# Feed-forward heads whose matmuls take w1 and w3 together, in units that hold two chunks of rows of both

## The chip, the cores and the metric

The kernel runs on one core of one Trainium2 chip. The metric is the device time of one execution in microseconds (us), less is better. Engines are named as in the profile: PE (TensorE, matmuls), PEld (its weight loads), DVE (VectorE), ACT (ScalarE), POOL (GpSimd) and SP (SyncE, which here only issues DMAs).

## The reference

One inference step of a diffusion backbone of two layers, on 384 tokens of 1024 numbers: 128 context tokens and 256 latent tokens, which is three tiles of 128 here. Each layer is a feed-forward half (FFN1), a token mixer (Fourier mixing, latent attention, neighbourhood attention, merged by gates and projected by `w_out`), and a second feed-forward half (FFN2). What the change touches is the feed-forward:

```python
def _modulate(x, shift, scale):
    return (_ln_plain(x) * (1.0 + scale) + shift)

def _swiglu(h, w1, w3, w2):                 # w1, w3: 1024 x 2816, w2: 2816 x 1024
    return (jax.nn.silu(h @ w1) * (h @ w3)) @ w2

def _ffn_sublayer(x, shift, scale, gate, w1, w3, w2, g, b):
    y = _swiglu(_modulate(x, shift, scale), w1, w3, w2)
    return _layernorm(ALPHA * x + 0.5 * gate * y, g, b)
```

All is fp32. The kernel splits each fp32 operand of a product into a high and a low part (fp32r) and adds three matmuls: high by high, high by low, low by high.

## The kernel before

The program is a row of sublayers: FFN1, mixer, FFN2, twice. Between two of them stands `transition(prev, nxt, mod)`: the old sublayer's last matmuls tile by tile (`tail(t)`: for a mixer the product with the eight chunks of `w_out`, tile `wo`; for a feed-forward the last eight chunks of w2, tile `y`), each followed by `res(t)` (gate, residual, layer norm; tiles `z`, `st`, and a square on ACT into `xn`), `norm(t)` (second normalisation; POOL's power into `st`, then `xn` on DVE) and `modu(t)` (transposes `xT` on PE, scale and shift into `hf` on DVE and ACT, then the split into `hmh` on ACT and `hml` on DVE). `modu(0)` stands within the last tail; `res(2)` and `norm(2)` ahead of the head; `modu(1)` and `modu(2)` after the first piece of the heads of tiles 0 and 1.

The **head** of a feed-forward is what follows: the first 512 of the 2816 columns of w1 and w3, in two groups `g` of 256, with the tokens as the stationary operand and the weights moving. For tile t and group g one PSUM bank `hd` holds h @ w1 in its first 256 columns and h @ w3 in its last 256; `sf` is then silu of the one times the other. The remaining columns come later, in `body`, with the weights stationary. The first sublayer of all has a head of its own (`cold_head`), which the change doesn't touch. The heads in question are three: T1 (mixer to FFN2, layer 0), T2 (FFN2 of layer 0 to FFN1 of layer 1) and T3 (mixer to FFN2, layer 1).

**Units and the planner.** Weights come in units. A unit is loaded by SP as raw fp32 (`raw`, line 180), cast by ACT to the high part (`whi`, line 188), and DVE subtracts to get the low part (`wlo`, line 193); each of the three takes a slot. There are two kinds of slot: `NU4` = 26 of 4 KB a partition and `NT3` = 22 of 3 KB; what has 768 words or fewer a partition goes into a 3 KB slot. Residual tiles, rows of the layer norm and gate, scratch tiles and most weight units take 4 KB slots. A first pass over the program, without emitting, notes when each unit is first and last used and a planned clock; `make_plan` and `place` then choose, unit by unit in order of first use, at which matmul its load and its two conversions are emitted: as early as wished (a lookahead in planned us) and as there is room among the slots in all the time until its last use. Conversions keep the order of first use. Where a unit finds no room, the lookahead of it and the ten before it shrink, and all is placed again:

```python
            for r in range(max(0, bad - 10), bad + 1):
                la[r] = (la[r][0] * 0.7, la[r][1] * 0.85)
```

SP issues its loads in the order in which they stand; one that waits for its slot (for the last reader of what was in it) holds up those behind it, and each also waits until the DMA eight before it has landed, on whose semaphore it counts. ACT, DVE and PE also run in program order.

Of the kernel before, what the change touches and what calls it, by code (L numbers as in the profile page):

```python
# [16 lines left out]
P = 128  # L17
D = 1024
KD = 8
# [1245 lines left out]
class FFN:  # L1265
# [13 lines left out]

    def w13(self, nme, g, c):  # L1280
        l, f, k = self.l, self.f, self.k
        n = 3 if g == 0 else 4
        i = c // n
        w = k.W((nme, l, f, g, i), f"ffn{f}_{nme}", l, i * n * P, min(n, KD - i * n), g * 256, 256)
        return tuple(x[:, c % n] for x in w)

    def head(self, t):
        k, nc = self.k, self.k.nc
        c = slice(t * P, (t + 1) * P)

        def piece(g, i):
            def go():
                if i == 0:
                    self.hb[t, g] = k.psum("hd")
                    if t == 0:
                        self.sf[g] = k.slot([P, NT, 256], F32, "sf")
                b = self.hb[t, g]
                for kk in range(KD):
                    k.mm3(b[:, i * 256:i * 256 + 256], (k.hm[0][:, kk, c], k.hm[1][:, kk, c]),
                          self.w13(("w1", "w3")[i], g, kk), kk == 0, kk == KD - 1)  # L1300
                if i == 1:
                    sf = self.sf[g][:, t]
                    nc.scalar.activation(out=sf, in_=b[:, 0:256], func=AF.Silu)
                    nc.vector.tensor_tensor(out=sf, in0=b[:, 256:512], in1=sf, op=ALU.mult)
            return go
        return [piece(g, i) for g in range(HG) for i in range(2)]
# [203 lines left out]
```

## Time and profile before

| | |
|---|---|
| median of 3 runs | 1886.09 us |
| lowest and highest | 1885.56 and 1888.81 us |
| the profiled execution | 1885.24 us |
| its span, first to last instruction | 1883.4 us |
| its mean granted PE clock | 0.997 |
| PE, PEld busy | 99%, 92% of the span |
| DVE, ACT, POOL busy | 71%, 42%, 7% of the span |
| DMA, mean over the span | 170 GB/s |

The busy time of PE is modelled from pipelined matmuls, so its share says that PE always has something, not that it is at its peak; how long a run of matmuls takes is read from the chain of waits, where the pieces follow each other. A timeline's row gives the start of an instruction or of a group of the same, its length, the engine, the line, the tiles and a count, and in brackets the idle time before it and what ended that. Line 77 is a helper that records most operations; tiles tell them apart.

### The profile page before, as it was taken

The page shows a single profiled execution, that of the slowest core. Times are in us where ns is not written, and L with a number is a line of the kernel's source. Part 1 is how long each engine was busy: PE and PEld are TensorE (multiplying, and loading weights), DVE is VectorE, ACT ScalarE, POOL GpSimd, SP SyncE. Part 2 cuts the span into 40 slices and gives each one's busy share as a digit, 9 for nine tenths or more (in the row PEclk, how much of TensorE's full clock was granted, in tenths as well). Part 3 has the DMA queues.
Part 4 walks back from the last instruction along what each step waited for, and adds up shares of the span by engine and source line. Part 5 has one row for each costly group of instructions (what it writes and reads, how often), then busy time and mean ns, then how long its engine had stood idle before and what let it go on. Part 6 is the DMA issues. An engine that isn't in the chain of part 4 may idle for free. (4 is left out here: it accounts for less than half of the span.)

```text
span 1883.4 us, 27546 instructions
## 1 busy us (share of the span) xinstructions
PE 1859.8 (99%) x10651; PEld 1726.4 (92%) x10651; DVE 1332.3 (71%) x2100; ACT 789.3 (42%) x1318; POOL 136.3 (7%) x287
## 2 busy tenths in 40 slices
PE   7999999999999999999999999999999999999997
PEld 5899998999999999999899999899999998999996
DVE  5776877688886676768775868778796876533344
ACT  4433335555365453323452333355554553533330
POOL 0000102000200000001000100220001000000000
PEclk9999999999999999999999999999999999999999
DMA  9865665234734456657555666543365354344522
GB/s 307 286 217 197 214 213 196 89 102 139 227 114 170 124 168 212 207 196 226 177 164 184 212 215 221 196 144 93 112 195 153 113 187 138 123 134 123 145 90 78
DMA packets 226243, 320.23 MB, mean 170 GB/s; under 512 B 33424, under 2 KB 182528, under 8 KB 225984
## 3 DMA queue, kind: packets, MB, share of 16 engines
q1 hardware_dynamic: 223616, 313.89, 51.9%
q0 software_dynamic: 2496, 4.59, 0.6%
q8 instruction: 83, 1.36, 0.3%
q14 instruction: 48, 0.39, 0.1%
HBM read 312.32 MB, written 8.02 MB: 170 GB/s over the span
## 5 line engine op out<-in xcount | busy, mean ns | idle before, releaser
L193 DVE TENSOR_TENSOR wlo<-raw,whi 128x1024 fp32r<-128x1024 f32 (+4 forms) x420 | 491.4, 1186 | 160.5 <-ACT whi L188 74.3
L188 ACT CAST whi<-raw 128x1024 fp32r<-128x1024 f32 (+4 forms) x420 | 421.1, 1021 | 369.3 <-DVE wlo L193 119.6
L77 PE MATMUL w<-hmh,whi 128*128 128x384 f32 x1152 | 386.7, 336 | 0.5 <-DVE sl L77 0.5
L77 PE MATMUL w<-hmh,wlo 128*128 128x384 f32 x1152 | 385.5, 335 | 0.0
L77 PE MATMUL w<-hml,whi 128*128 128x384 f32 x1152 | 385.2, 334 | 0.0
L77 PE MATMUL y<-whi,sT 128*128 128x512 f32 x1056 | 337.8, 391 | 0.7 <-DVE sT L77 0.4
L77 DVE SCALAR_TENSOR_TENSOR acc<-raw,cs,acc 128x1024 f32<-128x1024 f32 x236 | 295.3, 1286 | 11.9 <-DMA raw<-in_w_ada_dram 10.4
L77 PEld LDWEIGHTS y<-whi,sT 128*128 128x128 f32 x1056 | 197.9, 188 | 43.0 <-DVE sT L77 1.1
L77 PEld LDWEIGHTS w<-hmh,whi 128*128 128x128 f32 x1152 | 216.3, 188 | 12.1 <-issue 5.0
L77 PEld LDWEIGHTS w<-hml,whi 128*128 128x128 f32 x1152 | 216.3, 188 | 1.9
L77 PEld LDWEIGHTS w<-hmh,wlo 128*128 128x128 f32 x1152 | 216.2, 188 | 0.0
L77 PE MATMUL y<-wlo,sT 128*128 128x512 f32 x528 | 206.3, 391 | 0.0
L77 PE MATMUL g<-hmh,whi 128*128 128x384 f32 x384 | 131.9, 343 | 0.0
L77 PE MATMUL g<-hml,whi 128*128 128x384 f32 x384 | 129.1, 336 | 0.0
L77 PE MATMUL g<-hmh,wlo 128*128 128x384 f32 x384 | 129.1, 336 | 0.0
L77 PEld LDWEIGHTS y<-wlo,sT 128*128 128x128 f32 x528 | 99.1, 188 | 19.4
L77 ACT CAST sT<-sl 128x384 fp32r<-128x384 f32 x72 | 37.0, 514 | 159.8 <-DVE sl L77 159.8
L77 PE MATMUL hd<-whi,hmh 128*128 128x256 f32 (+1 forms) x336 | 101.1, 303 | 0.9 <-ACT hmh L77 0.7
L77 PE MATMUL hd<-wlo,hmh 128*128 128x256 f32 (+1 forms) x336 | 99.9, 299 | 0.0
L77 PE MATMUL hd<-whi,hml 128*128 128x256 f32 (+1 forms) x336 | 99.7, 299 | 0.0
L77 POOL TENSOR_TENSOR st<-st,mhalf 128x1 f32<-128x1 f32 x48 | 43.4, 906 | 662.9 <-DVE st L77 661.7
L77 DVE TENSOR_TENSOR sl<-w,sl 128x384 f32<-128x384 f32 x72 | 39.8, 553 | 52.3 <-PE w L77 52.0
(262 smaller groups left out, 2935.7 us busy)
## 6 DMA issues: line engine op xcount, KB each, us to landing
raw<-in_ffn_w_dram SPq DMA_DIRECT2D x244, 512.0 KB, 4.7
raw<-in_w_ada_dram SPq DMA_DIRECT2D x128, 512.0 KB, 5.0
raw<-in_w_gate_dram SPq DMA_DIRECT2D x48, 512.0 KB, 4.6
raw<-in_w_in_dram SPq DMA_DIRECT2D x32, 512.0 KB, 6.4
raw<-in_w_out_dram SPq DMA_DIRECT2D x16, 512.0 KB, 6.7
raw<-gd SPq DMA_DIRECT2D x12, 512.0 KB, 5.3
raw<-in_ffn_w_dram SPq DMA_DIRECT2D x22, 256.0 KB, 4.9
raw<-in_ffn_w_dram SPq DMA_DIRECT2D x12, 384.0 KB, 8.3
```

What stands on the lines that cost most here:

```text
L77: r = f(*a, **kw)
L188: self.real.scalar.copy(out=hi, in_=r)
L193: self.real.vector.tensor_tensor(out=lo, in0=r, in1=hi.bitcast(F32), op=ALU.subtract)
```

## The change

`w13` loses its case for group 0: its units all have four chunks now, and it serves the body alone. A new function `both(g, kk)` makes the head's units: each holds chunks 2i and 2i+1 of rows, of w1 and of w3, 256 columns each (2 x 2 x 256 = 1024 words a partition), filled by two DMAs of 256 KB, one from w1 and one from w3. Of the head's two pieces for a tile and a group, the first was w1 over all eight chunks and the second w3; now the first is chunks 0 to 3 and the second chunks 4 to 7, and each matmul writes all 512 columns of the bank. For a head that is 144 matmuls of 512 columns in the place of 288 of 256. Before, a head's ten units were, for group 0, six of three, three and two chunks of w1 and the same of w3 (768 or 512 words, 3 KB slots), and for group 1 four of four chunks (4 KB slots); now there are eight, all in 4 KB slots. In the program SP has 721 DMAs where it had 703, and ACT and DVE have two casts and two subtracts less per head.

```diff
@@ -1279,10 +1279,19 @@
 
     def w13(self, nme, g, c):
         l, f, k = self.l, self.f, self.k
-        n = 3 if g == 0 else 4
-        i = c // n
-        w = k.W((nme, l, f, g, i), f"ffn{f}_{nme}", l, i * n * P, min(n, KD - i * n), g * 256, 256)
-        return tuple(x[:, c % n] for x in w)
+        w = k.W((nme, l, f, g, c // 4), f"ffn{f}_{nme}", l, c // 4 * 4 * P, 4, g * 256, 256)
+        return tuple(x[:, c % 4] for x in w)
+
+    def both(self, g, kk):
+
+        l, f = self.l, self.f
+        i = kk // 2
+
+        def src(o):
+            return [((lambda t, x=x: t[:, :, x]), o.I[f"ffn{f}_{n}"][l, i * 2 * P:(i + 1) * 2 * P, g * 256:g * 256 + 256].rearrange("(a p) b -> p a b", p=P))
+                    for x, n in enumerate(("w1", "w3"))]
+        w = self.k.unit(("both", l, f, g, i), src, (2, 2, 256), True)
+        return tuple(x[:, kk % 2].rearrange("p a b -> p (a b)") for x in w)
 
     def head(self, t):
         k, nc = self.k, self.k.nc
@@ -1295,9 +1304,8 @@
                     if t == 0:
                         self.sf[g] = k.slot([P, NT, 256], F32, "sf")
                 b = self.hb[t, g]
-                for kk in range(KD):
-                    k.mm3(b[:, i * 256:i * 256 + 256], (k.hm[0][:, kk, c], k.hm[1][:, kk, c]),
-                          self.w13(("w1", "w3")[i], g, kk), kk == 0, kk == KD - 1)
+                for kk in range(4 * i, 4 * i + 4):
+                    k.mm3(b, (k.hm[0][:, kk, c], k.hm[1][:, kk, c]), self.both(g, kk), kk == 0, kk == KD - 1)
                 if i == 1:
                     sf = self.sf[g][:, t]
                     nc.scalar.activation(out=sf, in_=b[:, 0:256], func=AF.Silu)
```

The planner places the new units elsewhere. On SP at T1 there stood, before, the last three of the six units of group 0, then a unit of group 1, then the second and third residual rows (`xd`), then two units of group 1:

```order
L180 DMA raw_1174_6441<-in_ffn2_w3_dram 128x3x256
L180 DMA raw_1187_6475<-in_ffn2_w3_dram 128x3x256
L180 DMA raw_1188_6481<-in_ffn2_w3_dram 128x2x256
L180 DMA raw_1189_6486<-in_ffn2_w1_dram 128x4x256
L180 DMA raw_1190_6505<-xd_533_2955 128x1024
L180 DMA raw_1216_6624<-xd_534_2957 128x1024
L180 DMA raw_1217_6627<-in_ffn2_w1_dram 128x4x256
L180 DMA raw_1218_6629<-in_ffn2_w3_dram 128x4x256
```

Now the eight pairs stand between the second and the third residual row, of which these are the last four (raw_1200 holds chunks 0 and 1 of group 0, which PE needs first):

```order
L180 DMA raw_1199_6595<-in_ffn2_w1_dram 128x2x256
L180 DMA raw_1199_6595<-in_ffn2_w3_dram 128x2x256
L180 DMA raw_1200_6601<-in_ffn2_w1_dram 128x2x256
L180 DMA raw_1200_6601<-in_ffn2_w3_dram 128x2x256
L180 DMA raw_1201_6604<-in_ffn2_w1_dram 128x2x256
L180 DMA raw_1201_6604<-in_ffn2_w3_dram 128x2x256
L180 DMA raw_1202_6610<-in_ffn2_w1_dram 128x2x256
L180 DMA raw_1202_6610<-in_ffn2_w3_dram 128x2x256
L180 DMA raw_1203_6622<-xd_534_2957 128x1024
```

All the head's loads moved behind the second residual row, and the third residual row and the first-needed pair stand near their end.

On ACT at T1, before, six casts stand ahead of the residual steps (`xn` from `z` is a square for a variance, `hf` and `hmh` are the modulation of tile 0):

```order
L77 CAST mT_1163_6374<-g_1161_6357 128x384
L188 CAST whi_1191_6522<-raw_1171_6421 128x768
L188 CAST whi_1193_6531<-raw_1172_6428 128x768
L188 CAST whi_1205_6562<-raw_1173_6435 128x512
L188 CAST whi_1208_6587<-raw_1174_6441 128x768
L188 CAST whi_1210_6596<-raw_1187_6475 128x768
L188 CAST whi_1212_6604<-raw_1188_6481 128x512
L77 ACTIVATE xn_1178_6453,st_1177_6451<-z_1175_6445,st_1177_6451 128x1024
L77 ACTIVATE xn_1182_6463,st_1181_6461<-z_1175_6445,st_1181_6461 128x1024
L77 ACTIVATE xn_1198_6544,st_1197_6542<-z_1195_6536,st_1197_6542 128x1024
L77 ACTIVATE hf_1203_6557<-xT_1207_6567,mod_876_4681 128x128 x2
```

Now no cast of the head stands ahead of the modulation of tile 0:

```order
L77 ACTIVATE xn_1174_6445,st_1173_6443<-z_1171_6437,st_1173_6443 128x1024
L77 ACTIVATE xn_1178_6455,st_1177_6453<-z_1171_6437,st_1177_6453 128x1024
L77 ACTIVATE xn_1187_6522,st_1186_6520<-z_1184_6514,st_1186_6520 128x1024
L77 ACTIVATE hf_1192_6535<-xT_1194_6541,mod_876_4681 128x128 x2
L77 CAST hmh_1_65<-hf_1192_6535 128x4x128
L77 ACTIVATE hf_1192_6535<-xT_1194_6541,mod_876_4681 128x128 x2
L77 CAST hmh_1_65<-hf_1192_6535 128x4x128
L188 CAST whi_1204_6626<-raw_1200_6601 128x1024
L188 CAST whi_1206_6632<-raw_1196_6583 128x1024
L77 ACTIVATE xn_1209_6639,st_1208_6637<-z_1184_6514,st_1208_6637 128x1024
L77 ACTIVATE xn_1215_6654,st_1214_6652<-z_1212_6646,st_1214_6652 128x1024
L188 CAST whi_1220_6668<-raw_1197_6587 128x1024
```

The cast of the first-needed pair stands right behind it, and the casts of the later pairs behind the squares of tiles 1 and 2. On PE, the head of T1 began before with chunk 0 of w1 (whi_1191 is the cast of raw_1171):

```order
L77 MATMUL wo_1202_6553<-wlo_1158_6319,mT_1163_6374 128x512
L77 MATMUL wo_1202_6553<-whi_1157_6318,mT_1163_6374 128x512
L77 MATMUL hd_1236_6690<-whi_1191_6522,hmh_1_65 128x256
L77 MATMUL hd_1236_6690<-wlo_1192_6523,hmh_1_65 128x256
L77 MATMUL hd_1236_6690<-whi_1191_6522,hml_2_66 128x256
```

Now it begins with both matrices at once:

```order
L77 MATMUL wo_1191_6531<-wlo_1165_6388,mT_1159_6366 128x512
L77 MATMUL wo_1191_6531<-whi_1164_6387,mT_1159_6366 128x512
L77 MATMUL hd_1218_6662<-whi_1204_6626,hmh_1_65 128x512
L77 MATMUL hd_1218_6662<-wlo_1205_6627,hmh_1_65 128x512
L77 MATMUL hd_1218_6662<-whi_1204_6626,hml_2_66 128x512
```

The stationary tiles and their order are the same; the moving operand is twice as wide, and comes from the pair loaded sixth. On SP at T3, before, the loads of group 0 stand ahead of all rows and the order there is:

```order
L180 DMA raw_2679_15242<-in_ffn2_w3_dram 128x3x256
L180 DMA raw_2682_15257<-in_ffn2_w3_dram 128x2x256
L180 DMA raw_2683_15263<-in_ffn2_w1_dram 128x4x256
L180 DMA raw_2689_15322<-xd_2058_11924 128x1024
L180 DMA raw_2690_15324<-gd_1854_10785 128x1024
L180 DMA raw_2691_15326<-gd_1854_10785 128x1024
L180 DMA raw_2692_15328<-in_ln_g_dram 128x1024
L180 DMA raw_2693_15330<-in_ln_b_dram 128x1024
L180 DMA raw_2720_15434<-in_ffn2_w1_dram 128x4x256
L180 DMA raw_2721_15437<-xd_2059_11926 128x1024
L180 DMA raw_2733_15501<-in_ffn2_w3_dram 128x4x256
```

Now the pairs come after the second residual row:

```order
L180 DMA raw_2687_15118<-xd_2047_11630 128x1024
L180 DMA raw_2696_15148<-in_ffn2_w1_dram 128x2x256
L180 DMA raw_2696_15148<-in_ffn2_w3_dram 128x2x256
L180 DMA raw_2700_15183<-in_ffn2_w1_dram 128x2x256
L180 DMA raw_2700_15183<-in_ffn2_w3_dram 128x2x256
L180 DMA raw_2701_15188<-in_ffn2_w1_dram 128x2x256
L180 DMA raw_2701_15188<-in_ffn2_w3_dram 128x2x256
L180 DMA raw_2702_15197<-in_ffn2_w1_dram 128x2x256
L180 DMA raw_2702_15197<-in_ffn2_w3_dram 128x2x256
L180 DMA raw_2703_15206<-in_ffn2_w1_dram 128x2x256
L180 DMA raw_2703_15206<-in_ffn2_w3_dram 128x2x256
```

There raw_2702 holds chunks 0 and 1 of group 0, raw_2703 chunks 2 and 3, raw_2700 chunks 4 and 5 and raw_2701 chunks 6 and 7; raw_2696 belongs to group 1. At T2 the order is of the same kind: eight pairs in a row, and the first-needed is the fifth.

## Rows read from the trace of the kernel before

**Rows 1.** the page's part 1: busy us (share of the span) xinstructions

```profile
PE 1859.8 (99%) x10651; PEld 1726.4 (92%) x10651; DVE 1332.3 (71%) x2100; ACT 789.3 (42%) x1318; POOL 136.3 (7%) x287
```

**Rows 2.** PE's waits: who waited for whom, us, times, longest

```profile
PE hd L77 <- ACT hmh L77: 0.7, 1, 0.7
```

**Rows 3.** chain of waits, 1560 to 1660: start us, us, what

```profile
1595.82 2.87 PE hd L77 x24
1598.70 0.87 PE xT L77 x8
1599.57 11.51 PE hd L77 x96
```

**Rows 4.** chain of waits, 1181 to 1262, a run of 512-column matmuls

```profile
1248.78 5.48 PE uf L77 x24
```

**Rows 5.** timeline of SP (T1, T3): start us, us, what, xcount

```profile
665.00 0.34 SPq L180 DMA_DIRECT2D raw<-xd  x1
665.45 5.75 SPq L180 DMA_DIRECT2D raw<-in_ffn_w_dram  x6
...
1524.77 6.77 SPq L180 DMA_DIRECT2D raw<-in_ffn_w_dram  x6
...
1587.79 0.38 SPq L180 DMA_DIRECT2D raw<-in_ffn_w_dram  x1
1590.87 0.33 SPq L180 DMA_DIRECT2D raw<-xd  x1
```

**Rows 6.** timeline of PE: first hd matmul of T1 and T2

```profile
669.56 0.28 PE L77 MATMUL hd<-whi,hmh 128*128 128x256 f32 x1
...
953.49 0.28 PE L77 MATMUL hd<-whi,hmh 128*128 128x256 f32 x1
```

**Rows 7.** timeline of ACT, T3: start us, us, what, xcount

```profile
1563.95 4.08 ACT L188 CAST whi<-raw 128x768 fp32r<-128x768 f32 x6
```

**Rows 8.** groups by line and form: busy us, mean ns, idle before

```profile
L193 DVE TENSOR_TENSOR wlo<-raw,whi 128x1024 fp32r<-128x1024 f32 x376 | 455.7, 1225 | 160.3 <-ACT whi L188 74.1 <-PE w L77 29.8 <-issue 27.4
L188 ACT CAST whi<-raw 128x1024 fp32r<-128x1024 f32 x376 | 390.0, 1052 | 362.0 <-DVE wlo L193 117.9 <-PE w L77 80.7 <-DVE acc L77 61.7
...
L77 POOL TENSOR_TENSOR st<-st,mhalf 128x1 f32<-128x1 f32 x48 | 43.4, 906 | 662.9 <-DVE st L77 661.7 <-DVE sel L77 1.1
...
L77 DVE SCALAR_TENSOR_TENSOR z<-z,st,raw 128x1024 f32<-128x1024 f32 x30 | 38.4, 1279 | 2.0 <-POOL st L77 1.4 <-DMA raw<-in_ffn_w_dram 0.3
...
L77 DVE TENSOR_SCALAR hf<-xT,mod 128x128 f32<-128x128 f32 x60 | 20.9, 402 | 2.4 <-PE xT L77 2.4
...
L77 DVE TENSOR_TENSOR hml<-hf,hmh 128x512 fp32r<-128x512 f32 x30 | 20.2, 685 | 2.8 <-ACT hmh L77 2.4
...
L77 ACT CAST hmh<-hf 128x512 fp32r<-128x512 f32 x30 | 18.2, 620 | 2.6 <-DVE hf L77 2.3
...
L77 DVE TENSOR_SCALAR xn<-z,st,st 128x1024 f32<-128x1024 f32 x15 | 12.2, 813 | 8.1 <-POOL st L77 8.1
...
L77 DVE TENSOR_TENSOR sf<-hd,sf 128x256 f32<-128x256 f32 x24 | 9.5, 417 | 12.3 <-ACT sf L77 12.3
...
L77 DVE SCALAR_TENSOR_TENSOR z<-wo,raw 128x512 f32<-128x512 f32 x12 | 8.1, 687 | 9.0 <-PE wo L77 8.9
```

**Rows 9.** all DMA issues: KB each, median us to landing

```profile
raw<-in_ffn_w_dram SPq DMA_DIRECT2D x22, 256.0 KB, 4.9
raw<-in_ffn_w_dram SPq DMA_DIRECT2D x12, 384.0 KB, 8.3
...
raw<-in_w_branch_m_dram SPq DMA_DIRECT2D x8, 512.0 KB, 4.0
```

**Rows 10.** windows, T3: us, busy PE PEld DVE ACT POOL, PEclk, DMA, GB/s

```profile
1595.60:1612.00 16.40, 16.40 (x139) 16.36 (x139) 13.48 (x27) 7.86 (x15) 2.00 (x2) 1.00 0.69 226
```

**Rows 11.** windows: the kernel's end; columns as in rows 10

```profile
1870.00:1875.00 5.00, 3.90 (x18) 2.89 (x16) 1.68 (x3) 0.00 (x0) 0.00 (x0) 1.00 0.00 0
...
1880.00:1883.00 3.00, 0.00 (x0) 0.00 (x0) 0.00 (x0) 0.00 (x0) 0.00 (x0) 0.50 0.27 98
```

## Prediction

> **What bounds the kernel now.** I read the page's first part first: TensorE (PE) is busy 1859.8 us of 1883.4, VectorE (DVE) 71%, ScalarE (ACT) 42% [rows 1]. Then PE's waits: of all the head matmuls (tile hd) one waited, for 0.7 us [rows 2]. Then the chain of waits, which through the heads is PE alone: hd matmuls back to back, with only the xT transposes between them [rows 3]. So before the change every weight of a head is there in time, and two things decide: how long PE needs for a head, and whether the weights and the modulated tiles still come in time once their loads and conversions stand elsewhere.
>
> **PE's own gain.** A run of 96 hd matmuls of 256 columns takes 11.51 us [rows 3], 0.1199 us each. A matmul of 512 columns takes 5.48/24 = 0.2283 us [rows 4]. Two become one: 2 x 0.1199 - 0.2283 = 0.0115 us. Each head has 3 tiles x 2 column groups x 2 matrices x 8 chunks x 3 products = 288 matmuls of 256 that become 144 of 512; three heads change (mixer to second FFN in layer 0, second FFN to the next layer's first, mixer to second FFN in layer 1; T1, T2, T3 below). 432 x 0.0115 = 4.9 us saved, all on the path. A page speaks to the size: the Trainium skill, "TensorE: Matmul & The Clock Gate", Part 1, section "Wait — 56ns, not 53.3ns?", gives a matmul at full clock a fixed cost of about 2.5 ns beside its columns. By that the saving would be 432 x 2.5 ns, an estimate of 1.1 us, and the sum 3.8 us higher; the row says more than four times as much, and I go by the row.
>
> **What the planner does with the new units.** Before, each head's first column group came in six units of 768 or 512 words a partition, which live in the 22 slots of 3 KB, apart from the 26 slots of 4 KB that everything else crowds into. In T3, for example, they were loaded from 1524.77 on [rows 5] and cast from 1563.95 on [rows 7] for a head that begins at 1595.82 [rows 3]; the heads of T1 and T2 begin at 669.56 and 953.49 [rows 6]. Now all eight units of a head have 1024 words and want three 4 KB slots each while rows, residual tiles and the last w_out or w2 chunks still hold these. The order shows the result: in T1 all eight units' loads, each now two DMAs, stand behind the second residual row, and the pair that PE needs first (raw_1200, chunks 0 and 1) is the sixth; ACT's six early casts are gone, and the casts stand after the modulation of tile 0. In T2 the pair needed first is the fifth. In T3 it is the fourth, and the pair needed second the fifth. Two conversions less per head (1.05 + 1.23 us each [rows 8]) are work off the path; I give them nothing beyond the count below.
>
> **When the first pair comes.** SP waits for each slot's last reader, and the loads behind it wait too. In T1 and T2 the slots come free one by one as the last 24 matmuls of the tail read their chunks for the last time. The first is free 21 matmuls before the head, 21 x 0.228 = 4.8 us: at 664.8 in T1, where the old kernel's xd load, waiting for the matmul beside it, went out at 665.00, the next 0.45 later [rows 5], and at 948.7 in T2. Three pairs go ahead, six issues of 0.45 = 2.7 us; the needed pair's second DMA is one more behind: 667.9 and 951.9. Landing takes a median of 4.9 us for 256 KB [rows 9]: 672.8 and 956.8; the cast 1.05 [rows 8]. First matmul at 673.9 and 957.8 against 669.56 and 953.49: 4.3 us late each. Bounds: the quickest weight loads land in 4.0 us, the 384 KB loads, which come in bursts as these will, in 8.3 [rows 9]: 3.4 to 7.7 us late. I take 4.9, the row of the same size. In T3 the first pair waits for what released the 1587.79 load [rows 5] and is in time; the second waits, as the xd load at 1590.87 did: 1591.3 + 4.9 + 1.05 = 1597.25.
>
> **What DVE then has to do.** From the first cast on, before tile 1's matmuls can begin, DVE must run, in this order of program: 8 subtracts (8 x 1.225 = 9.8), four half-row residual steps (4 x 0.69 = 2.75), two layer-norm steps (2 x 1.28 = 2.56), xn of tile 1 (0.81), the four modulation steps that fall to it (4 x 0.40 = 1.61) and sf (0.42): 17.95 us, then ACT's cast hmh (0.62): 18.6 us [rows 8]. PE's work over that stretch is 48 matmuls x 0.2283 + 0.87 for xT [rows 3, 4] = 11.84. So 6.7 us are lost, whatever the loads do: DVE becomes the bound of the first third of the head. Before, most of these subtracts lay ahead, and DVE was already busy 13.48 of 16.40 us there [rows 10]; with four more subtracts it would need 18.4, more than the stretch has. Behind it xn of tile 2 (POOL 0.91 + DVE 0.81, against a cast and two matmuls, 1.08) costs 0.65 and hml (2 x 0.69 against 0.87) 0.5: 1.1 us. In T3 DVE may start at 1594.15, 1.5 us ahead of PE's first need, but stands idle from 1595.4 to 1597.25 for the second pair: 6.7 - 1.5 + 1.85 + 1.1 = 8.2 us. The xd row of tile 2 also comes later in T1 and T3, since it stands behind all pairs (T1: issue at about 672 instead of 665.00); it lands about when DVE turns to it, so I count nothing, up to 3 us. From tile 1's matmuls on, everything of the head is there and PE runs through; nothing gives the time back, because PE has no slack later [rows 1].
>
> **Other edits.** 18 DMA issues more, 18 x 0.45 = 8 us of SP time in places where SP waits for slots anyway: only those counted above matter. Later conversions of w_out 5 to 7 and of w2: nothing, as their use follows by more than one cast and subtract (2.3 us); at most that, once per transition. PSUM: one bank per tile and group as before, nothing.
>
> **Sum.** T1 4.3 + 6.7 + 1.1 = 12.1; T2 the same; T3 8.2; together 32.4 - 4.9 = +27.5 us. The profiled execution took 1885.24, 0.85 under the median: 1912.7, forecast 1913 us.
>
> **Rivals.**
> (a) The loads and conversions hide and only PE's gain is left: 1885.2 - 4.9 = 1880, faster. It decides where a pair's load goes out at least 7.2 us before its first matmul (4.9 + 1.05 + 1.23). For it: no hd matmul waits today, and SP issues when slots free, not when the planner thinks. Against: the slots' last readers are the tail's own last matmuls, so nothing can go out early, and the casts and subtracts must follow.
> (b) Only the late first pairs cost, DVE keeps up: 4.3 + 4.3 + 1.9 - 4.9 = +5.6 to half the sum, 1891 to 1902. For it: my DVE list is serial, and part of the residual steps may run while the first pair is awaited.
> (c) PE's idle lowers its clock. In the last stretches of the kernel PE has run out of work, and the granted clock goes from 1.00 to 0.50 of full, that is from 2.4 to 1.2 GHz [rows 11]. The idle 4.3 us at the heads of T1 and T2 could do the same. The twelve matmuls behind each would take 2 x 2.74 us, +2.7; if the gaps that follow keep the clock low until tile 1, 11.84 us of PE work become 23.7, against DVE's 18.6: +5.1. Both heads, and T3 at half of it: +7 to +13, so 1920 to 1926. The Trainium skill, same page, Part 1, section "What's actually happening", says the same in kind: throttled is the default and activity releases it; the trace agrees at its end. Against: PE restarts at once here, and its gaps after the first are short.
> (d) A matmul of 512 here isn't cheaper than two of 256: +4.9, inside the range.
>
> **Chances.** The forecast's neighbourhood (1903 to 1920) 0.50, (b) 0.19, (c) with slow landings (1920 to 1934) 0.15, above that 0.03, (a) 0.09, within 0.2% of before 0.04. 0.2%, 3.8 us, is about what a measurement of this kernel can tell from no change. The range leaves out (a), no change and the far end: 1891 to 1934. Faster 0.09, same 0.04, slower 0.87.
>
> **What would show it.** Right: PE's waits list hd for whi and wlo with some 25 to 35 us in all; PE idle of about 4 us at the start of T1's and T2's heads with a landing as the releaser, in T3 about 2; DVE busy without gaps for 18 us in each; 144 hd matmuls of 512 columns at 0.228 us. Wrong: hd matmuls that wait for nothing (a); waits that end with the first pair (b); a granted clock of 0.5 inside the heads (c); later stages slower than before, which I don't expect, would mean that the planner's other moves cost. The forecast falls most easily at DVE's 18.6 us, if its residual steps run while the first pair is still on its way.

## The result and the profile after

The kernel after takes 1918.71 us in the median of four runs (1916.82 to 1920.04), the kernel before, on the same chip, 1885.82 (1884.68 to 1888.81): ratio 1.0174, 95% interval 1.0162 to 1.0186. The change costs 32.9 us; the forecast was 1913, some 28 us slower than the profiled execution before. The profiled execution of after has a span of 1914.9 us and a mean granted clock of 0.992, against 1883.4 and 0.997.

The page's part 1, after (compare [rows 1]):

```profile
PE 1868.7 (98%) x10219; PEld 1708.7 (89%) x10219; DVE 1334.6 (70%) x2094; ACT 786.7 (41%) x1312; POOL 136.8 (7%) x287
```

PE has 432 instructions fewer, as the diff says, and is nevertheless "busy" 9 us longer; matmuls at half clock, shown below, are part of that. No engine has more instructions; most of the time is in waiting. PE's waits, after (total us, times, longest; compare [rows 2], where hd waits once, for 0.7 us, and that in the first sublayer's own head, at 18 us):

```profile
PE hd L77 <- ACT whi L188: 16.7, 6, 5.3
...
PE hd L77 <- DVE wlo L193: 3.1, 4, 1.1
```

To see where the 33 us go I measure each head from the moment at which its first matmul could start (0.23 us behind the start of the tail's last one) to the first matmul of `body` (tile `w`). For T1 that first matmul of `body` is, before and after:

```profile
706.00 0.34 PE L77 MATMUL w<-hmh,whi 128*128 128x384 f32 x1
```

```profile
718.20 0.33 PE L77 MATMUL w<-hmh,whi 128*128 128x384 f32 x1
```

Before, T1, T2 and T3 take 36.44, 36.27 and 36.27 us (T1 from 669.56 [rows 6]). With the cheaper matmuls alone each would take 1.65 us less (144 x 0.0115), about 34.65. After, they take 48.28, 49.12 and 42.77 (T1 from 669.92): losses of 13.6, 14.5 and 8.1 us. Minus the 4.9 saved that is 31 of the 31.6 us between the two profiled executions; no other stretch of the program moves by more than 0.8 us. The profiled execution of after is the fastest of its four, which is why the medians are 1.3 us further apart.

**T1.** SP and PE of after (start us, us, what; in brackets the idle time before and its releaser):

```profile
659.89 11.54 SPq L180 DMA_DIRECT2D raw<-in_ffn_w_dram  x16
...
665.12 3.95 SPq L180 DMA_DIRECT2D raw<-in_ffn_w_dram  x8
...
672.09 0.34 SPq L180 DMA_DIRECT2D raw<-xd  x1
```

```profile
669.69 0.39 PE L77 MATMUL wo<-whi,mT 128*128 128x512 f32 x1
675.32 0.79 PE L77 MATMUL hd<-whi,hmh 128*128 128x512 f32 x1 [5.25 <-ACT whi L188]
...
677.60 0.63 PE L77 MATMUL hd<-whi,hmh 128*128 128x512 f32 x1
...
681.01 0.63 PE L77 MATMUL hd<-whi,hml 128*128 128x512 f32 x1
...
683.59 0.50 PE L77 MATMUL hd<-whi,hmh 128*128 128x512 f32 x1 [0.79 <-ACT whi L188]
685.18 0.53 PE L77 MATMUL hd<-wlo,hmh 128*128 128x512 f32 x1 [1.09 <-DVE wlo L193]
...
694.84 0.41 PE L77 MATMUL hd<-whi,hmh 128*128 128x512 f32 x1
```

The sixteen loads of the head go out between 659.9 and 671.4, all but the last two within the tail; the second row of SP is the fifth to the twelfth of them alone (the third to the sixth pair), which after a stop go out some 0.5 us apart. PE runs out of work at 670.1 and waits 5.25 us for the cast of the first pair. ACT's cast waited for the landing, and DVE for the cast:

```profile
674.23 1.99 ACT L188 CAST whi<-raw 128x1024 fp32r<-128x1024 f32 x2 [10.30 <-DMA raw<-in_ffn_w_dram]
```

```profile
675.30 2.36 DVE L193 TENSOR_TENSOR wlo<-raw,whi 128x1024 fp32r<-128x1024 f32 x2 [10.10 <-ACT whi L188]
...
682.64 0.15 DVE L77 TENSOR_SCALAR st<-st 128x1 f32<-128x1 f32 x1 [1.37 <-ACT xn L77]
...
692.33 1.37 DVE L77 TENSOR_SCALAR hf<-xT,mod 128x128 f32<-128x128 f32 x4
```

DVE stands idle for 10 us, while the loads come, and then works 18 us with one gap until the modulation of tile 1 is out at 693.7; tile 1's first matmul is the row at 694.84. From the first hd matmul to it PE takes 19.5 us for 11.84 us of work.

**T2** has the same shape. PE, DVE and ACT of after:

```profile
971.86 0.79 PE L77 MATMUL hd<-whi,hmh 128*128 128x512 f32 x1 [5.35 <-ACT whi L188]
...
984.11 0.50 PE L77 MATMUL hd<-whi,hmh 128*128 128x512 f32 x1 [1.92 <-ACT whi L188]
985.69 0.64 PE L77 MATMUL hd<-wlo,hmh 128*128 128x512 f32 x1 [1.08 <-DVE wlo L193]
...
992.40 0.50 PE L77 MATMUL hd<-whi,hmh 128*128 128x512 f32 x1 [0.98 <-ACT hmh L77]
```

```profile
983.15 0.15 DVE L77 TENSOR_SCALAR st<-st 128x1 f32<-128x1 f32 x1 [1.37 <-ACT xn L77]
...
991.88 0.42 DVE L77 TENSOR_TENSOR sf<-hd,sf 128x256 f32<-128x256 f32 x1 [0.82 <-ACT sf L77]
```

```profile
991.46 0.38 ACT L77 ACTIVATE sf<-hd 128x256 f32<-128x256 f32 x1 [3.47 <-PE hd L77]
```

Here DVE's list has three gaps, 2.6 us together (the first of them, 0.44, is a wait for POOL at 978.77). In the first two DVE waits for steps of its own chain on POOL and ACT. The third goes back to PE: ACT's `sf` waits 3.47 us for the last matmuls of tile 0, and the second cast `hmh` of tile 1 stands behind it. PE takes 20.5 us to tile 1.

**T3** begins without a wait, but the chain of waits leaves PE there (after, 1595 to 1670; compare [rows 3], where it is PE throughout):

```profile
1611.41 9.33 PE wo L77 x42
1620.74 6.10 DMA raw<-xd
```

```profile
1626.94 0.69 DVE L77 SCALAR_TENSOR_TENSOR z<-raw,z 128x512 f32<-128x512 f32 x1 [0.81 <-DMA raw<-xd]
```

```profile
1628.60 1.15 ACT L77 ACTIVATE xn<-z,st 128x1024 f32<-128x1024 f32 x1 [4.97 <-DVE st L77]
```

```profile
1630.83 0.66 PE L77 MATMUL hd<-whi,hmh 128*128 128x512 f32 x1 [3.07 <-ACT whi L188]
```

The third residual row's load (xd), issued behind the sixteen pair loads, ends last, and then the work on it: DVE's residual step waits for the row, ACT's square for DVE, and PE for a cast that stands behind that square.

### The profile page after: what moved, and what is told of

The parts are those of the page before. It is cut to its first block, busy times and chain, and to the rows that moved or that the text cites. A ratio compares the mean times of both kernels' runs of the same rounds, so it can differ in the third digit from the quotient of the medians.

```text
span 1914.9 us, 26708 instructions
## 1 busy us (share of the span) xinstructions
PE 1868.7 (98%) x10219; PEld 1708.7 (89%) x10219; DVE 1334.6 (70%) x2094; ACT 786.7 (41%) x1312; POOL 136.8 (7%) x287
## 5 line engine op out<-in xcount | busy, mean ns | idle before, releaser
L193 DVE TENSOR_TENSOR wlo<-raw,whi 128x1024 fp32r<-128x1024 f32 (+3 forms) x414 | 492.5, 1205 | 176.3 <-ACT whi L188 90.5
L188 ACT CAST whi<-raw 128x1024 fp32r<-128x1024 f32 (+3 forms) x414 | 420.0, 1032 | 383.6 <-DVE wlo L193 130.0
L77 DVE SCALAR_TENSOR_TENSOR acc<-raw,cs,acc 128x1024 f32<-128x1024 f32 x236 | 295.1, 1285 | 19.5 <-DMA raw<-in_w_ada_dram 15.6
L77 PEld LDWEIGHTS y<-wlo,sT 128*128 128x128 f32 x528 | 99.1, 188 | 19.4
L77 PE MATMUL hd<-whi,hmh 128*128 128x512 f32 x192 | 80.1, 422 | 18.8 <-ACT whi L188 16.7
L77 PE MATMUL hd<-wlo,hmh 128*128 128x512 f32 x192 | 78.5, 412 | 3.1 <-DVE wlo L193 3.1
L77 ACT ACTIVATE xn<-z,st 128x1024 f32<-128x1024 f32 x30 | 34.6, 1153 | 107.5 <-DVE st L77 85.4
L77 PE MATMUL hd<-whi,hml 128*128 128x512 f32 x192 | 77.8, 409 | 0.4 <-DVE hml L77 0.4
```

What stands on the lines that cost most here:

```text
L77: r = f(*a, **kw)
L188: self.real.scalar.copy(out=hi, in_=r)
L193: self.real.vector.tensor_tensor(out=lo, in0=r, in1=hi.bitcast(F32), op=ALU.subtract)
```

## The experiments

The runs part the units from the matmuls (e1, e2), DVE from the clock (e5, e6), the order of the loads from DVE (e4, e8, e9, e11), and the kind of slot from all of these (e3, e7, e10). Times below are medians beside runs of the kernel before on the same chip.

| kernel | us | minus before | ratio (95%) |
|---|---|---|---|
| after | 1918.71 | +32.9 | 1.0174 (1.0162 to 1.0186) |
| e1_cols256 | 1921.35 | +35.6 | 1.0184 (1.0170 to 1.0198) |
| e2_group1 | 1883.21 | -2.6 | 0.9986 (0.9977 to 0.9994) |
| e5_light | 1912.52 | +26.8 | 1.0137 (1.0122 to 1.0152) |
| e6_warm | 1921.23 | +35.6 | 1.0181 (1.0165 to 1.0196) |
| e4_sorted | 1914.97 | +29.2 | 1.0147 (1.0133 to 1.0160) |
| e8_row | 1917.06 | +31.4 | 1.0164 (1.0147 to 1.0181) |
| e9_rowsorted | 1904.11 | +18.4 | 1.0091 (1.0076 to 1.0106) |
| e11_rowlight | 1896.59 | +10.6 | 1.0055 (1.0041 to 1.0068) |
| e3_onechunk | 1889.80 | +4.0 | 1.0019 (1.0010 to 1.0028) |
| e7_u29 | 1915.04 | +29.0 | 1.0157 (1.0143 to 1.0171) |
| e10_packed | 1880.93 | -5.1 | 0.9975 (0.9965 to 0.9985) |

### Units or matmuls: e1_cols256 and e2_group1

e1 keeps the new units and goes back to two matmuls of 256 columns.

```diff
-                    k.mm3(b, (k.hm[0][:, kk, c], k.hm[1][:, kk, c]), self.both(g, kk), kk == 0, kk == KD - 1)
+                    w = self.both(g, kk)
+                    for x in range(2):
+                        s = slice(x * 256, x * 256 + 256)
+                        k.mm3(b[:, s], (k.hm[0][:, kk, c], k.hm[1][:, kk, c]), tuple(y[:, s] for y in w),
+                              kk == 0 and x == 0, kk == KD - 1 and x == 1)
```

> The units of two chunks of both matrices stay, with their loads and conversions; only the matmuls go back to 256 columns. Theory (the units' late loads and conversions make the loss; in the first third of each head DVE is the bound and hides PE): of the 4.9 us that 512 columns save only two thirds lie on the path, so 3.3 us over the changed kernel, 1922. Rival 1 (PE's saving is additive): 4.9 us over it, 1923.6. Rival 2 (the wide matmuls cause the waits, the units are harmless): back to 1886 to 1890.

It took 2.6 us more than after (by the two ratios to before, 1.9; the heads of its trace are 3.0 us longer). The loss is all still there without the wide matmuls: it is the units'. Of the 4.9 us that the wide ones save, 1.9 to 3.0 is on the path, which fits a head whose first third is set by something else than PE; the intervals exclude neither the expected 3.3 nor rival 1's 4.9.

e2 gives group 0 its old units and narrow matmuls back, and leaves the pairs and the 512 columns in group 1.

```diff
...
-                for kk in range(4 * i, 4 * i + 4):
-                    k.mm3(b, (k.hm[0][:, kk, c], k.hm[1][:, kk, c]), self.both(g, kk), kk == 0, kk == KD - 1)
+                if g == 0:
+                    for kk in range(KD):
+                        k.mm3(b[:, i * 256:i * 256 + 256], (k.hm[0][:, kk, c], k.hm[1][:, kk, c]),
+                              self.w13(("w1", "w3")[i], g, kk), kk == 0, kk == KD - 1)
+                else:
+                    for kk in range(4 * i, 4 * i + 4):
+                        k.mm3(b, (k.hm[0][:, kk, c], k.hm[1][:, kk, c]), self.both(g, kk), kk == 0, kk == KD - 1)
```

> Half of the change alone: column group 0 keeps its six units in 3 KB slots and matmuls of 256 columns, group 1 gets units of both matrices and 512 columns (four 4 KB units before and after). Theory: the planner finds the old places, no head waits, and 3 x 72 matmul pairs save 216 x 0.0115 = 2.5 us: 1883.3. Rival (pairs of DMAs, or needing both matrices of a chunk at once, cost by themselves): waits at group 1 of some us per head, 1888 to 1896.

2.6 us faster than before, as expected. PE's waits in e2:

```profile
PE hd L77 <- ACT hmh L77: 0.7, 1, 0.7
```

That is [rows 2] again. 216 pairs of matmuls became one each: 2.6 us / 216 = 11.9 ns each, against 11.5 by the rows. The interval of the ratio allows 1.1 to 4.3 us, so this confirms that there is a gain and its rough size, no more; in the profiled execution the three heads are 1.4 us shorter, as two new waits of 0.4 us for `xn` take part of it back. The whole loss sits in the units of group 0, which left the 3 KB slots.

### DVE or the clock: e5_light and e6_warm

e5 makes the low part of the pairs with an operation that takes 0.69 us instead of 1.23.

```diff
-        self.real.vector.tensor_tensor(out=lo, in0=r, in1=hi.bitcast(F32), op=ALU.subtract)
+        if self.units[i]["key"][0] == "both":
+            self.real.vector.tensor_scalar(out=lo, in0=hi.bitcast(F32), scalar1=2.0 ** -13, scalar2=None, op0=ALU.mult)
+        else:
+            self.real.vector.tensor_tensor(out=lo, in0=r, in1=hi.bitcast(F32), op=ALU.subtract)
```

> The changed kernel, but in the heads' units DVE makes the low part as the high part times 2^-13, which is not the low part: one input instead of two, about 0.81 us instead of 1.22, after the same cast. Theory (DVE is the bound of the first third of each head): 8 x 0.41 = 3.3 us less per head, in T3 less since DVE waits there for a row: 6 to 9 us under the changed kernel, 1910 to 1913. Rival (the waits are for loads and for ACT's queue, DVE has room): at most 2 us less, 1917.

6.2 us less than after: 24 subtracts lost 24 x 0.54 = 13 us of DVE time, and about half came back on the path (in the heads of the profiled execution only 3.4 us; the first waits there are half a microsecond longer). DVE is a bound of the heads; the waits for whi stay (17.6 us in all), so it is not the only one. In T1 the next bound is PE itself. ACT in T1, and the window there (columns as in [rows 10]):

```profile
687.89 0.38 ACT L77 ACTIVATE sf<-hd 128x256 f32<-128x256 f32 x1 [1.36 <-PE hd L77]
```

```profile
684.00:686.00 2.00, 2.00 (x6) 1.61 (x5) 2.00 (x6) 1.98 (x3) 0.00 (x0) 0.50 0.00 0
```

From 683.49 to tile 1's first matmul at 693.25 PE never waits, the first eight matmuls of that run at half clock, and ACT waits for PE.

e6 puts twenty matmuls without a purpose into PE's wait at the heads of T1 and T2, to keep the clock up; all other instructions stay where they are.

```diff
+                if t == 0 and g == 0 and i == 0 and (self.l, self.f) != (1, 2) and k.plan is not None:
+                    for j in range(20):
+                        k.real.tensor.matmul(b, lhsT=k.hm[0][:, j % 8, c], rhs=k.hm[0][:, 4 * (j % 2):4 * (j % 2) + 4, c], start=True, stop=True)
```

> The changed kernel with 20 needless matmuls of 512 columns (4.6 us) on PE at the start of the heads of T1 and T2, where PE waits 5.3 us anyway; their result is overwritten. Theory (DVE is the bound while the granted clock is 0.5, so the clock costs little): 0 to 4 us less than the changed kernel, 1915 to 1919. Rival (the lowered clock costs what PE's matmuls take longer, some 3 us right behind the wait and 2 later, per head): 8 to 10 us less, 1909 to 1911.

The clock had indeed fallen in after. Windows of after, T1 (us; then length, busy of PE, PEld, DVE, ACT, POOL; granted clock; DMA share; GB/s):

```profile
676.00:682.00 6.00, 5.54 (x15) 4.25 (x15) 5.17 (x11) 2.00 (x4) 0.55 (x1) 0.50 0.20 76
...
683.00:685.00 2.00, 0.50 (x1) 0.19 (x1) 2.00 (x2) 2.00 (x3) 1.39 (x1) 1.00 0.00 0
...
686.00:688.00 2.00, 2.00 (x6) 1.59 (x5) 2.00 (x4) 1.98 (x3) 0.00 (x0) 0.50 0.00 0
...
689.00:694.00 5.00, 5.00 (x24) 4.12 (x23) 4.85 (x10) 4.17 (x9) 0.06 (x1) 1.00 0.61 170
```

In e6's timeline of PE the first twelve hd matmuls run at full clock (0.39 to 0.50 us where after has 0.63 to 0.80):

```profile
670.14 4.70 PE L1309 MATMUL hd<-hmh 128*128 128x512 f32 x20
675.77 0.50 PE L77 MATMUL hd<-whi,hmh 128*128 128x512 f32 x1 [0.93 <-ACT whi L188]
...
684.04 0.80 PE L77 MATMUL hd<-whi,hmh 128*128 128x512 f32 x1 [2.65 <-ACT whi L188]
```

PE is then earlier at the next pair and waits 2.65 us there instead of 0.79; the head takes 48.94 us against 48.28 (T2 49.44 against 49.12), and the kernel is not faster: it took 2.5 us more than after, above what either side expected; the two intervals overlap, and why it is more was not taken apart. So the half clock of the first twelve matmuls costs nothing here: PE would wait in any case. The second stretch at half clock, 684 to 690, e6 did not remove. In T1 of after it can cost next to nothing, for DVE works without a gap from 682.64 to 693.7 and the cast hmh behind it ends 0.13 us before tile 1's first matmul at 694.84: there the two bounds are level. In T2 the last gap of DVE's list is a wait for PE, whose matmuls from 985.7 to 989.1 run at half clock; had they not, the second cast hmh, at 991.74, could have followed DVE's hf, which ends at 990.39, some 1.3 us earlier (an estimate from these two times; no run tested it). And e5 shows that the clock does cost once DVE is relieved.

### The order of the loads: e4_sorted, e8_row and e9_rowsorted, e11_rowlight

The eight pairs' loads keep their eight places in the program; e4 deals them out in the order of first use. e8 exchanges the third residual row's load with the earliest pair's. e9 does both.

```diff
+        heads = {}
+        for i in order:
+            if self.units[i]["key"][0] == "both":
+                heads.setdefault(self.units[i]["key"][1:3], []).append(i)
+        for h in heads.values():
+            for i, d in zip(h, sorted(self.units[i]["d"] for i in h)):
+                self.units[i]["d"] = d
```

> The changed kernel with the load times of a head's eight units dealt out anew in order of first use, so that the pair needed first is loaded first; conversions stay where they are. Theory: the two long first waits (5.3 us each in T1 and T2) go, DVE starts its list some 6 us earlier in T1 and T2 but remains the bound there (18.6 us of DVE against 11.8 of PE): 12 to 15 us less than the changed kernel, 1904 to 1907. Rival 1 (the lowered clock after the long idle is most of the loss): with no idle nothing is left of T1 and T2, some 26 us less, 1893. Rival 2 (the order doesn't matter, slots come free too late for all): 0 to 3 us less, 1916 to 1919.

Only 3.7 us less than after (its four runs range from 1910.1 to 1916.2): mostly a miss. T2's first wait is gone (its head takes 43.9 us, 5.2 less), but in T1 the wait moved one step down. PE, DVE, ACT and SP of e4:

```profile
681.49 0.79 PE L77 MATMUL hd<-whi,hmh 128*128 128x512 f32 x1 [8.38 <-ACT whi L188]
```

```profile
677.61 0.69 DVE L77 SCALAR_TENSOR_TENSOR z<-raw,z 128x512 f32<-128x512 f32 x1 [5.64 <-DMA raw<-xd]
```

```profile
679.26 1.15 ACT L77 ACTIVATE xn<-z,st 128x1024 f32<-128x1024 f32 x1 [9.74 <-DVE st L77]
...
680.41 3.87 ACT L188 CAST whi<-raw 128x1024 fp32r<-128x1024 f32 x4
```

```profile
659.11 11.52 SPq L180 DMA_DIRECT2D raw<-in_ffn_w_dram  x16
671.03 0.48 SPq L180 DMA_DIRECT2D raw<-xd  x1
```

Read from the bottom up: the row goes out at 671.03, behind the sixteen pair loads; DVE's residual step waits for it until 677.61, ACT's square of that result stands in ACT's order ahead of the casts, and so four casts of pairs whose loads had all gone out by 670.6 are held up until 680.41. T3 has the same wait, 4.83 us.

```diff
+        for l in range(DEPTH):
+            h = [i for i in order if self.units[i]["key"][:3] == ("both", l, 2)]
+            r = self.byk[("xr", l, 2)]
+            i = min(h, key=lambda i: self.units[i]["d"])
+            a, b = self.units[r], self.units[i]
+            if b["d"] < a["d"] <= b["s"]:
+                a["d"], b["d"] = b["d"], a["d"]
```

> The changed kernel with the load of the third residual row (T1, T3) put ahead of the eight pairs, in exchange with the first of them; the pairs keep their order otherwise. Theory as the sorted loads have changed it (the row behind the pairs holds up ACT's square, and with it the casts behind it, but in T1 DVE and the late first pair hide that): T3 loses its wait of 3 us, T1 0 to 2: 3 to 5 us under the changed kernel, 1914 to 1916. Rival (the row is what bounds both heads): 8 us or more less, 1910.

1.6 us less: a miss by about 1, which is within the noise of the two medians. With the first pair still late, the row alone is worth little.

e9 is e4 with two lines more (`f == 2` are T1 and T3):

```diff
+            if f == 2:
+                h.insert(0, self.byk[("xr", l, 2)])
```

> Both: the third residual row first, then the eight pairs in order of first use. Theory (three causes one behind the other: the late first pair, the row behind the pairs, and DVE's 18.6 us of work): with the first two gone DVE starts at once and is left as the bound: T1 loses 6 us instead of 13.5, T2 7 instead of 14.5, T3 3 instead of 8: 1885.8 - 4.9 + 16 = 1897. Rival 1 (DVE is no bound): 1885 to 1889. Rival 2 (the room, not the order, makes the loss): 1910 or more.

14.6 us less than after, two to three times e4 and e8 added (3.7 + 1.6 = 5.3 by the medians, 7.0 by the ratios): each of the two hid what the other would have given. The heads now begin at once and lose 7.5, 9.3 and 6.1 us. The effect is T1's: there e4 gained 1.0 us, e8 0.3 and e9 6.2. In T2, where no row is moved, e9 gains what e4 gained, 5.2; in T3 e9 gains 2.0. It is not the 1897 that was expected. PE and DVE of e9 in T1:

```profile
678.08 0.79 PE L77 MATMUL hd<-whi,hmh 128*128 128x512 f32 x1 [2.65 <-ACT whi L188]
```

```profile
669.33 1.23 DVE L193 TENSOR_TENSOR wlo<-raw,whi 128x1024 fp32r<-128x1024 f32 x1 [3.05 <-ACT whi L188]
...
687.19 1.36 DVE L77 TENSOR_SCALAR hf<-xT,mod 128x128 f32<-128x128 f32 x4
```

From 669.33 to 688.55 DVE needs 19.2 us for the list that the prediction had put at 18 us, with a gap of 1.37 us for ACT's square as in after; the wait of 2.65 us is for a cast that stands behind ACT's square of the third row's result, and that behind DVE. What is left after the loads have been mended is DVE's list with its detour over ACT.

e11 is e9 with e5's cheaper low part.

> The kernel with the third residual row first and the pairs sorted (1904), with the cheaper stand-in for the low part in the heads (the high part times 2^-13, which is not the low part; 0.81 us instead of 1.22). Theory (with the loads in order DVE's list is what is left): 3 us less per head, 7 to 9 in all, 1895 to 1897. Rival (what is left is room for the later pairs or ACT's queue): at most 3 us less, 1901 to 1904.

7.5 us less than e9, within the expectation. Mending the loads and making the subtracts cheaper takes 22 of the 33 us away; the remaining 11, and the 4.9 us that the wide matmuls should give, were not taken apart. Waits for casts (5.2 us in e11) are part of them.

### The slots: e3_onechunk, e7_u29 and e10_packed

e3 makes the pairs of group 0 half as large, one chunk each (512 words, 3 KB slots).

```diff
-        i = kk // 2
+        m = 1 if g == 0 else 2
+        i = kk // m
...
-        w = self.k.unit(("both", l, f, g, i), src, (2, 2, 256), True)
+        w = self.k.unit(("both", l, f, g, i), src, (m, 2, 256), True)
```

> All matmuls of 512 columns, but group 0's units hold one chunk of both matrices (512 words a partition, so they go into the 3 KB slots), eight of them; group 1 as in the changed kernel. Theory (what cost was the room: in 4 KB slots the units came late): loads and conversions go ahead of the head again, no hd waits beyond 1 us, and all 4.9 us are gained: 1881. Rival 1 (16 more small DMAs and two more conversions per head bring waits): 1886 to 1892. Rival 2 (one pair of DMAs per unit is what made the loads late): as slow as the changed kernel, 1915 or more.

1889.80: it takes 29 of the 33 us away, but not all that was expected; the number lies where rival 1 put it. The heads take 35.02, 36.93 and 40.13 us: T1 is good, T3 is not. PE in T3 of e3:

```profile
1598.30 0.50 PE L77 MATMUL hd<-wlo,hmh 128*128 128x512 f32 x1 [1.04 <-DVE wlo L193]
...
1600.04 0.51 PE L77 MATMUL hd<-wlo,hmh 128*128 128x512 f32 x1 [0.76 <-DVE wlo L193]
```

The high and low parts of eight units hold 16 of the 22 small slots where those of six held 12, beside their raw parts and what the mixer keeps there; the planner again put loads and conversions close to the head. SP and ACT of e3 ahead of T3, whose head begins at 1596.87 (in T3 the six loads of before stood at 1524.77 [rows 5], for a head at about the same time):

```profile
1563.31 15.79 SPq L180 DMA_DIRECT2D raw<-in_ffn_w_dram  x12
```

```profile
1594.70 0.61 ACT L188 CAST whi<-raw 128x512 fp32r<-128x512 f32 x1
```

The first cast stands 2 us ahead of the head, where before it stood 32 us ahead [rows 7]. e3 doesn't part the room from rival 1; e10, whose group 0 takes as many small DMAs, speaks against the DMAs, and the two more conversions stay untested.

e7 keeps the change and turns four small slots into three large ones.

```diff
-NU4 = 26
-NT3 = 22
+NU4 = 29
+NT3 = 18
```

> The changed kernel with 29 slots of 4 KB and 18 of 3 KB instead of 26 and 22; nothing else. The planner then loads and converts two pairs of T1 and three of T3 24 us ahead, and T2's first pairs some 3 us earlier. Theory (room in 4 KB slots is the root): first pairs in time in T1 and T3, DVE relieved of two and three subtracts there: 10 to 18 us under the changed kernel, 1901 to 1909. Rival (the order of loads and DVE matter, not room): 1915 or more.

1915.04, a miss. The heads did get better, with losses of 6.2, 7.6 and 2.5 us where after has 13.6, 14.5 and 8.1, 20 us in all; but the stretches ahead of T1 and T3, with the mixers in them, got longer by 11.3 and 7.3 us. PE's waits in e7:

```profile
PE uf L77 <- DVE wlo L193: 5.1, 3, 2.5
PE g L77 <- DVE qN L77: 2.5, 1, 2.5
```

T1's head begins at 681.18, 11 us after PE was ready for it in after. 16 of the 20 us went back. That they went because the mixers miss the four small slots is likely but not shown: these waits are only 7.6 of the 18.6 us, and the rest was not taken apart.

e10 packs group 0 into six units of the old sizes. A piece (x, c) is chunk c of w1 (x = 0) or w3 (x = 1); pieces that lie side by side in one unit make one matmul of 512 columns, chunks 1 and 4, whose halves lie in two units, two of 256. Group 1 stays as in after.

```diff
+    PACK = (((0, 0), (1, 0), (0, 1)), ((1, 1), (0, 2), (1, 2)), ((0, 3), (1, 3), (0, 4)), ((1, 4), (0, 5), (1, 5)),
+            ((0, 6), (1, 6)), ((0, 7), (1, 7)))
...
-                for kk in range(4 * i, 4 * i + 4):
-                    k.mm3(b, (k.hm[0][:, kk, c], k.hm[1][:, kk, c]), self.both(g, kk), kk == 0, kk == KD - 1)
+                if g == 0:
+                    for kk in range(4 * i, 4 * i + 4):
+                        for s, w in self.packed(kk):
+                            k.mm3(b[:, s], (k.hm[0][:, kk, c], k.hm[1][:, kk, c]), w, kk == 0, kk == KD - 1)
...
```

> Group 0 in six units of the old sizes (three or two blocks of 256 columns) that live in the 3 KB slots, but packed in order of chunks: w1 and w3 of chunk 0 with w1 of chunk 1, then w3 of chunk 1 with both of chunk 2, and so on. Six of eight chunks of group 0 and all of group 1 then take matmuls of 512 columns, two chunks two of 256. Theory (only the room in 4 KB slots hurt; with the old sizes the old places are found): 3 x 126 x 0.0115 = 4.3 us under before, 1881.4, and no hd waits. Rival (needing both matrices of a chunk at once, 16 DMAs of 128 KB instead of six, or DVE, brings waits): 1884 to 1890.

1880.93 us, 5.1 less than before and 38 less than after: the fastest kernel here. SP and ACT of e10 ahead of T1, whose head begins at 667.12:

```profile
631.90 14.37 SPq L180 DMA_DIRECT2D raw<-in_ffn_w_dram  x18
```

```profile
644.62 0.62 ACT L188 CAST whi<-raw 128x512 fp32r<-128x512 f32 x1 [0.33 <-DMA raw<-in_ffn_w_dram]
```

The six units are loaded from 631.90 on, 35 us ahead of their use instead of 10, and cast by 645.2; the two rows go out behind them but in time. The one hd wait of 0.7 us is again that of the first sublayer's head, and the three heads take 34.78, 35.46 and 34.76 us, close to the 34.65 of the working. By the prediction's price 378 pairs x 0.0115 = 4.3 us; 5.1 was measured (by the interval of the ratio 2.8 to 6.6).

## Why the prediction was right

Direction and cause were right: the units cost (e1, e2, e10), PE's own gain is what the rows said (e2), and the forecast was 6 us short, inside the range. By its steps:

- **PE's own gain, 4.9 us.** Right as far as it was measured: 2.6 us in e2 where 2.5 was priced, 5.1 in e10 where 4.3 was. The fixed cost of about 2.5 ns a matmul, from the Trainium skill, "TensorE: Matmul & The Clock Gate", Part 1, section "Wait — 56ns, not 53.3ns?", does not agree: by it e2 would have gained an estimated 0.5 us, and it gained 2.6 (interval of the ratio 0.9977 to 0.9994, so 1.1 to 4.3).
- **The first pair, 4.3 us late in T1 and in T2.** Mis-sized: 5.4 and 5.5, from the moment at which the first matmul could start. In T1 it came at 675.32 instead of 673.9, of which 0.4 us is that PE came later to the head (669.92 against 669.56) and so is no loss. The rest is the load. The time at which the slots come free was right for the third pair: the prediction's 664.8 for the first of four pairs is the row of eight loads at 665.12; two pairs had gone out before, which it doesn't say. The needed pair's second DMA is the last of the eight, at about 668.6 instead of 667.9, and the cast began at 674.23, so that landing took some 5.6 us instead of 4.9.
- **DVE's list, 18.6 us.** Right as a list, short by its gaps: from 675.3 to the end of hmh at 694.7 it takes 19.4 in T1 with a gap of 1.37, and 20.5 in T2 with the three gaps above. The prediction added up DVE's operations as if none waited for POOL and ACT, which have steps of the same chain, or, as the last one in T2, by way of ACT for PE. The first third so lost 7.7 us in T1 and 8.7 in T2 against 6.7. These 1.0 and 2.0 us, with the 2.3 us of the two first pairs and less at the later xn and hml (0.5 and 0.3 against 1.1), are the mis-sized part: T1 and T2 were put at 12.1 each and lost 13.6 and 14.5. That is 3.9 of the 4.1 us between 1912.7 and the 1916.82 of the profiled execution after. The sign that the prediction named, DVE busy without gaps, so did not come; nor did the 25 to 35 us of hd waits for whi and wlo: they are 19.8, and matmuls at half clock fill part of the rest.
- **T3, 8.2 us.** 8.1 measured, but not by the way told. The prediction had DVE idle for the second pair; the trace has a wait of 3.07 us for casts which stand behind ACT's square of the third residual row's result, and the chain goes over that row. The right size there is partly luck.
- **The xd row, "I count nothing, up to 3 us".** In T1 right as the change stands: DVE comes to the row and finds it there. In T3 DVE waits 0.81 us for it. But the step took the row as a cost of its own size, and it isn't: with the first wait taken away (e4) the row holds PE up for 8.4 us in T1 and 4.8 in T3. The causes are stacked; each is hidden by the one above.
- **Rival (c), the clock.** It happened, in T1, T2 and T3, with a granted clock of 0.50; but the 2.7 us for the first twelve matmuls, which the rival put on top, were not paid (e6), since DVE and the casts set the pace, and the clock did not stay low until tile 1: in T1 it was 1.00 from 689 on. It did fall a second time within the heads, as the rival allowed, and in T2 that held up the last piece of DVE's list; the sum has no term for it.
- **Rivals (a), (b) and (d).** No hd wait, first pairs only, 512 no cheaper: excluded by the waits, by e5 and by e2.
- **"Nothing gives the time back" and the later stages.** Right: outside the heads the profiled program moves by less than 1 us.

## What to carry to other kernels

Where a planner places loads by slots, the size class of a unit decides how early it can come: regrouping data moves it from a pool with room into one without, and the price, here some 36 us in the heads against a gain of 5, is paid far from the edited line. A better shape of matmul can be had without that, if the pieces are packed into units of the old sizes (e10). And where several late things stand behind each other (a load, a row, a cast behind a square, a subtract), taking one away shows the next: only pairs of fixes tell what each is worth (e9 against e4 and e8).

## What the runs showed of the hardware

The clock fell after short gaps too (granted clock and lengths of the matmuls in the rows above and below). In T1 of after it is 1.00 again at 683 to 685, then PE waits 0.79 and 1.09 us with one matmul between, and the next ones are granted 0.50; the same follows two gaps of 1.04 and 0.76 us in T3 of e3, where no longer wait stands ahead. Windows of e3:

```profile
1598.00:1600.00 2.00, 0.98 (x3) 0.49 (x3) 2.00 (x5) 0.34 (x1) 0.00 (x0) 1.00 0.90 249
1600.00:1604.00 4.00, 3.96 (x11) 3.03 (x12) 4.00 (x10) 3.86 (x7) 0.86 (x1) 0.59 1.07 384
```

The prediction had taken gaps of that size for harmless. At half clock (1.2 GHz) 512-column matmuls follow each other every 0.427 us (eight from 677.60 to 681.01 in T1 of after), at full (2.4 GHz) every 0.228 [rows 4], which is 1.87 times and not the 2 by which the prediction priced it.
